# PSUM banks in rotation for Strassen products, and a longer lead of gate steps ahead of stick-breaking attention

## The chip, the cores and the metric

The kernel runs on one core of a Trainium2 chip. The metric is the device time of one execution in microseconds (us), the median of several runs; lower is better. Engines are named as the profile names them: PE is TensorE (PEld its weight loads, which run beside matmuls), DVE VectorE, ACT ScalarE, POOL GpSimd and SP SyncE.

## The reference

A decoder trunk of two layers works on one sequence of 512 positions, 2048 wide, in f32. Layer 0 is sparse attention: an indexer scores keys, the top 128 of them are kept per query, and softmax attention with 16 heads over 4 key/value groups follows, gated by SiLU. Between the layers keys and values are computed once (`shared_kv`); layer 1 attends to them by stick-breaking. Each layer ends with an output projection, a layer norm, and a gated embedding. What the change touches, cut to its core:

```python
def shared_kv(x, w_kv):
    k, v = jnp.split(x @ w_kv, [KVW_B], axis=-1)
    ...
def mixer_b(x, w_in, w_o, k, v):
    q, gate = jnp.split(x @ w_in, [WIDTH_B], axis=-1)
    ...
        z = jnp.einsum('bqngd,bsnd->bngqs', qg, k).astype(jnp.float32) * (HEAD_DIM ** -0.5)
        strict = key_pos[None, :] < t[:, None]
        log_om = jnp.where(strict, -jax.nn.softplus(z), 0.0)
        suffix = lax.cumsum(log_om, axis=log_om.ndim - 1, reverse=True) - log_om
        a = jnp.where(strict, jnp.exp(jax.nn.log_sigmoid(z) + suffix), 0.0)
        o = jnp.einsum('bngqs,bsnd->bqngd', a.astype(v.dtype), v)
    ...
    return (o * jax.nn.silu(gate)) @ w_o
```

## The kernel before, in words

**Precision.** Every f32 factor is split into a high part (rounded by ACT, `wh`, `xh`, `qh`, `sh`, `ah`) and a low part (the rest, a DVE subtraction, `wl`, `xl`, `ql`, `sl`, `al`). A product is three matmuls, high·high, high·low and low·high: `mm3`, L133, whose three matmuls carry the lines 134 to 136. Weights come by DMA from SP's queue into three buffers `raw` of two 128-row blocks each, and are split one or two blocks ahead of use (`plain_items`, L219).

**Order of work.** TensorE's instructions run in the order in which the program issues them (`manual_schedule`). On ACT and DVE a scheduler orders the instructions, except those that are pinned to the program's order. PSUM is eight banks of 128 × 512 f32, named by number through `bank(i)`, L126; a bank that is used again waits for its last reader. `interleave`, L57, mixes two generators on TensorE: first `lead` steps of the second, then, at every yield of the first, as many of the second as bring it to its share of `n_fill`; what is left comes at the end.

**Around the change.** Layer 0 ends with `finish_layer` (L731), whose embedding gate is computed in chunks of 512, 512, 256 and 256 columns, each in banks listed at L924. Then follow:

1. The keys (L970 to L974): a product of 16 k-blocks in four banks, copied by ACT into `Kf` (tile E in the profile).
2. Five chunks of Strassen products (L984 to L999), the values first and then four chunks of queries into the tiles `f`. `gemm_s` (L328) computes for each k-pair and each of two rows seven products of three 256-wide matmuls, in the bank order `M` = m1, m2, m6, m7, m5, m3, m4, one bank each; a pass over the seven products is 21 matmuls. When a chunk is done, `combine` (L351) empties the banks: ACT copies m1 (into `u`), m7 and m5, DVE adds m2 and u, m6 and u, then (a step later) the sum of the copies, m3, and m4. The next chunk's matmuls on a bank wait for that. During the second chunk the values are transposed on TensorE, four times four 128 × 128 blocks (`turn_values`, L977), in a bank that the chunk leaves free; ACT copies them back.
3. DVE and ACT split keys, values and queries (`kl`, `vl`, `ql`), and DVE makes two triangular constants (`neg`, `tri`, L1005 to L1010).
4. Four groups g of stick-breaking attention (L1113 to L1123). `sticks` (L1046) goes through ten units (i, kb) of a 128-query block and a 128-key block, each in three stages: `logits` makes z with three matmuls, softplus on ACT and DVE, and the split `sh`, `sl`; `weights` adds the suffix sums on TensorE (L1086, z from `neg`, `tri`), then exp on ACT and the split `ah`, `al`; `values` multiplies by the values into o. Step s issues logits of unit s, weights of unit s − 1, values of unit s − 2. `interleave` fills the waits with the group's gate product: 64 gate steps, one k-block and one of banks 0 to 3 each, three matmuls 512 wide (g). Group 0 has 20 gate steps ahead of its first logits and 40 more over 34 yields, the other groups 8 and 52. Behind each group ACT loads the table for SiLU, and gates.

Line 111 is the helper through which every ACT and DVE instruction goes, so the profile's groups are told apart by tile.

Of the kernel before, what the change touches and what calls it, by code (L numbers as in the profile page):

```python
# [56 lines left out]
def interleave(main, n_main, fill, n_fill, lead=0):  # L57

    steps(fill, lead)
    done = 0  # L60
    for i, _ in enumerate(main, 1):
        steps(fill, n_fill * i // n_main - done)
        done = n_fill * i // n_main
    run(fill)
# [13 lines left out]
def trunk_kernel(  # L78
# [47 lines left out]
    def bank(i, name="ps"):  # L126
        return psum.tile([128, 512], F32, name=name, tag=f"bank{i}")
# [118 lines left out]
    def gemm_w(items, get, banks, n=512, order=range(NK)):  # L246

        for i, kb in enumerate(order):
            wh, wl = next(items)
            x = get(kb)  # L250
            for j, out in enumerate(banks):
                a, b = j * 128, min(n, (j + 1) * 128)
                mm3(out[: b - a], (wh[:, a:b], wl[:, a:b]), x, i == 0, i == len(order) - 1)
                yield
# [67 lines left out]
    def strassen_stream(widths, wp):  # L322
        return Ahead(strassen_items(widths, wp), 2)

    def product_banks():
        return [bank(i, f"m{i}").rearrange("p (j t) -> p j t", j=2) for i in range(7)]

    def gemm_s(items, C3, M):  # L328

# [160 lines left out]
    items = plain_stream((512, NK, True), (80, NK, False), *[(512, NK, False)] * 11)  # L490
# [51 lines left out]
    banks = mm_banks("iq")  # L542
# [5 lines left out]
    ps = bank(7, "ik")  # L548
# [15 lines left out]
    banks = mm_banks("iq")  # L564
# [32 lines left out]
    banks = mm_banks("k")  # L597
# [52 lines left out]
    banks = [bank(b, "v") for b in (4, 5, 6, 7)]  # L650
# [11 lines left out]
    Q = split_queries(0)  # L662
# [68 lines left out]
    def finish_layer(layer, resid, last, keep, early, ahead):  # L731
# [179 lines left out]
        with tc.tile_pool(name=f"pe{layer}", bufs=1, side="right") as ep:  # L911

            def gated(n, b):
                sg = ep.tile([128, T], F32, name="sg", tag="sg", bufs=4)
                act.activation(sg, b, AF.Sigmoid)
                dve.tensor_tensor(sg, sg, E[n], ALU.mult)
                dve.tensor_tensor(fblock(n), fblock(n), sg, ALU.add)

            def store(n, k):
                rows = last[n * 128 : (n + k) * 128, :].rearrange("(j p) t -> p j t", p=128)  # L920
                nc.sync.dma_start(rows, F[n // 4][:, n % 4 : n % 4 + k])

            first = 0
            for c, (n, where) in enumerate(((512, (2, 3, 4, 5)), (512, (6, 7, 0, 1)), (256, (2, 3)), (256, (0, 1)), (0, ()))):  # L924
                for j, b in enumerate(banks):
                    bg.append(lambda n=first + j, b=b: gated(n, b))
                    if j % 2:
                        bg.append(lambda n=first + j - 1: store(n, 2))
                first += len(banks)
                if first == 12:  # L930
                    bg.extend(early)
                if not n:
                    break
                banks = [bank(b, "g") for b in where]
                gemm = pumped(gemm_w(gitems, plain, banks, n), 4 if n == 512 else 2)
                if c == 3:
                    steps(gemm, 18)
                    ahead(gemm)
                run(gemm)
                drain()  # L940
            drain()
# [25 lines left out]
    with ps_:  # L967
        sp = ps_.enter_context(tc.tile_pool(name="sp1", bufs=1))
        C3.extend(c3_tiles(sp, range(4, 8)))
        Kf, Vf = shared[0][:, 0:4], shared[0][:, 4:8]  # L970
        banks = [bank(b, "k") for b in (4, 5, 6, 7)]
        gemm = gemm_w(kitems, plain, banks, order=PAIRS)
        items = first_chunk(gemm, TF, T1, C3, lambda: strassen_stream([512] * 5, sp))
        for g in range(4):  # L974
            act.activation(Kf[:, g], banks[g], AF.Copy)

        def turn_values(t):  # L977
            s = slice(t * 128, (t + 1) * 128)
            ps = bank(7, "vt")
            for g in range(4):  # L980
                pe.transpose(ps[:, g * 128 : (g + 1) * 128], Vf[:, g, s], ident)
            act.activation(Vf[:, :, s], ps.rearrange("p (g d) -> p g d", g=4), AF.Copy)

        for n, dst in enumerate((Vf, *F)):  # L984
            M = product_banks()
            gemm = pumped(gemm_s(items, C3, M), 8)
            if n == 1:
                steps(gemm, 40)
                for t in range(4):
                    steps(gemm, 16)  # L990
                    turn_values(t)
            run(gemm)
            drain()
            if n == 4:
                for k in range(8):
                    if k % 4 == 0:
                        raw = next_raw()
                    split(XH[k][:, H:T], XL[k][:, H:T], raw[:, k % 4])
            bg.extend(combine(sp, M, lambda i: quarter(dst, i)))  # L999
        drain()  # L1000
# [31 lines left out]
    Q = split_scaled(0)  # L1032
# [13 lines left out]
    def sticks(g, Q):  # L1046
        units = [(i, kb) for i in range(4) for kb in range(i, -1, -1)]
        later = {}
        running = {}
        state = {}  # L1050
        out = {}

        def logits(u):
            i, kb = units[u]
            z = spare("z")
            ks = slice(kb * 128, (kb + 1) * 128)
            mm3(z, [k[:, ks] for k in K[g]], Q[i], True, True)
            e = work()
            keep = kb == i > 1
            sp = px.tile([128, 512], F32, name="run", tag="run", bufs=2) if keep else work()  # L1060
            act.activation(e, z, AF.Abs)
            act.activation(e, e, AF.Exp, scale=-1.0)
            act.activation(e, e, AF.Ln, bias=1.0)
            dve.scalar_tensor_tensor(sp, z, 0.0, e, ALU.max, ALU.add)
            if kb == i:
                strict(sp)
            parts = tuple(px.tile([128, 512], F32R, name=f"s{s}", tag=f"s{s}", bufs=4) for s in "hl")
            split(*parts, sp)
            state[u] = z, parts
            if keep:  # L1070
                running[i] = sp
            if kb == i:
                later[u + 1] = parts
            elif kb:
                below = tuple(px.tile([128, 512], F32R, name=f"r{s}", tag=f"s{s}", bufs=4) for s in "hl")
                dve.tensor_tensor(running[i], running[i], sp, ALU.add)
                dve.tensor_copy(below[0], running[i])
                dve.tensor_tensor(below[1], running[i], below[0].bitcast(F32), ALU.subtract)
                later[u + 1] = below

        def weights(u):
            i, kb = units[u]
            z, parts = state[u]
            terms = [(neg, p) for p in (later[u] if kb < i else ())] + [(tri, p) for p in parts]
            for n, (m, p) in enumerate(terms, 1):
                pe.matmul(z, m, p, start=False, stop=n == len(terms), skip_group_check=True)  # L1086
            a = work()
            act.activation(a, z, AF.Exp)
            if kb == i:
                strict(a)  # L1090
            parts = tuple(px.tile([128, 512], F32R, name=f"a{s}", tag=f"a{s}", bufs=2) for s in "hl")
            split(*parts, a)
            state[u] = parts

        def values(u):
            i, kb = units[u]
            if kb == i:
                out[i] = bank(7, "o")
            mm3(out[i], [v[:, g] for v in V[kb]], state.pop(u), kb == i, kb == 0)
            if kb == 0:  # L1100
                act.activation(F[g][:, :, i * 128 : (i + 1) * 128], out[i].rearrange("p (h q) -> p h q", h=4), AF.Copy)

        for s in range(12):
            for fn, u in ((logits, s), (weights, s - 1), (values, s - 2)):
                if s == 1 and fn == weights:
                    for _ in range(4):
                        yield
                if 0 <= u < 10:
                    fn(u)
                    yield  # L1110

    for g in range(4):
        tc.keep_in_program_order(act.preload_act_table_set("natural_log_exp_and_others"))  # L1113
        banks = mm_banks("g")
        interleave(sticks(g, Q), 30 + 4, gemm_w(items, plain, banks), 52 - 12 * (g == 0), lead=8 + 12 * (g == 0))
        if g < 3:
            Q = split_scaled(g + 1)
        for h in range(4):
            sg = work()
            act.activation(sg, banks[h], AF.Silu)  # L1120
            dve.tensor_tensor(F[g][:, h], F[g][:, h], sg, ALU.mult)
# [51 lines left out]
```

## Time and profile before

| what | value |
| --- | --- |
| median of 3 runs | 1927.42 us (1927.31 to 1927.74) |
| the profiled execution | 1927.01 us |
| its span in the trace | 1925.3 us |
| granted TensorE clock, mean | 0.997 |
| Strassen chunks begin at | 1066.8, 1107.1, 1150.5, 1192.0, 1233.7 us; the last ends at 1275.2 |
| group 0: first logits, last values matmuls | 1289.7, 1342.7 us |

Rows of the profile's timeline read: start, duration, engine, line, operation, written tile <- read tiles, shapes, count, and in brackets the idle time before and what ended it. A matmul's duration includes its passage through the array, and matmuls overlap, so the pitch between starts is what a matmul costs; a wait shows as a start that comes late. Rows of the waits read: the engine and its tile and line, what it waited for, and then the total, the number of times and the longest. Rows of the windows read: from and to, length, then the busy time and count of PE, PEld, DVE and ACT, the granted clock, and DMA share and rate.

### The profile page before, as it was taken

What the parts mean: (1) busy time and instruction counts of PE and PEld (TensorE: products, weight loads), DVE (VectorE), ACT (ScalarE), POOL (GpSimd) and SP (SyncE); (2) the same over time, 40 slices, a digit from 0 to 9 for tenths busy, and PEclk for the clock granted to TensorE, in tenths of its full rate; (3) what the DMA queues carried; (4) which work ended last, traced back from release to release, by engine and by line L of the source; (5) the groups of instructions that cost most, each with busy time, mean ns of one, the idle gap of its engine ahead of it and who ended that gap; (6) DMA issues with size and microseconds to landing.
All of it is one profiled execution on the core that took longest, in us unless ns stands there. A gap on an engine that the chain in (4) does not pass through costs nothing.

```text
span 1925.3 us, 25105 instructions
## 1 busy us (share of the span) xinstructions
PE 1901.7 (99%) x9223; PEld 1590.5 (83%) x9223; DVE 1226.8 (64%) x2378; ACT 932.6 (48%) x1697; POOL 45.3 (2%) x61
## 2 busy tenths in 40 slices
PE   8999999999999999999999999999999999999998
PEld 7778888888888888877888999987888888887887
DVE  6677667985566445576357788876656645568434
ACT  4345222355555433375235444458877743347323
POOL 0110000000000000000000000011100000000000
PEclk9999999999999999999999999999999999999999
DMA  6322333322222342233334333331222152242333
GB/s 195 99 77 75 93 96 98 99 77 66 66 66 67 121 142 88 88 120 112 119 112 123 106 99 100 104 116 46 70 71 64 58 180 94 81 127 88 121 99 110
DMA packets 108301, 189.24 MB, mean 98 GB/s; under 512 B 8256, under 2 KB 25664, under 8 KB 108176
## 3 DMA queue, kind: packets, MB, share of 16 engines
q1 hardware_dynamic: 108032, 187.33, 31.4%
q8 instruction: 72, 1.18, 0.3%
q14 instruction: 53, 0.43, 0.1%
q0 software_dynamic: 144, 0.30, 0.1%
HBM read 179.21 MB, written 8.39 MB: 97 GB/s over the span
## 4 chain that ended last, share of the span: by engine, by line
PE 92%; DVE 4%; ACT 1%; DMA 1%; issue 1%; POOL 0%; SPq 0%; DVEq 0%; ACTq 0%
PE g L135 12%; PE g L134 12%; PE g L136 12%; PE o L135 7%; PE o L136 7%; PE o L134 7%; PE m L134 3%; PE m L135 3%; PE m L136 3%; PE q L135 3%; PE q L136 3%; PE q L134 3%; PE z L1086 2%; PE k L135 1%; PE k L134 1%; PE k L136 1%
## 5 line engine op out<-in xcount | busy, mean ns | idle before, releaser
L111 DVE TENSOR_TENSOR wl<-raw,wh 128x512 fp32r<-128x512 f32 (+2 forms) x692 | 432.8, 627 | 469.0 <-ACT wh L111 455.1
L111 ACT ACTIVATE wh<-raw 128x512 fp32r<-128x512 f32 (+2 forms) x692 | 397.8, 576 | 678.7 <-PE g L135 245.5
L134 PE MATMUL g<-xh,wh 128*128 128x512 f32 x1024 | 404.8, 395 | 0.4 <-ACT u L111 0.3
L135 PE MATMUL g<-xl,wh 128*128 128x512 f32 x1024 | 402.0, 393 | 2.1 <-DVE xl L111 2.1
L136 PE MATMUL g<-xh,wl 128*128 128x512 f32 x1024 | 400.7, 391 | 1.3 <-DVE wl L111 1.3
L135 PEld LDWEIGHTS g<-xl,wh 128*128 128x128 f32 x1024 | 192.6, 188 | 44.7 <-DVE xl L111 6.5
L136 PEld LDWEIGHTS g<-xh,wl 128*128 128x128 f32 x1024 | 192.4, 188 | 42.2 <-DVE wl L111 1.8
L134 PEld LDWEIGHTS g<-xh,wh 128*128 128x128 f32 x1024 | 192.9, 188 | 41.5 <-ACT sg L111 1.9
L136 PE MATMUL o<-xh,wl 128*128 128x512 f32 x512 | 199.3, 389 | 0.0
L135 PE MATMUL o<-xl,wh 128*128 128x512 f32 x512 | 199.3, 389 | 0.0
L134 PE MATMUL o<-xh,wh 128*128 128x512 f32 x512 | 199.2, 389 | 0.0
L136 PEld LDWEIGHTS o<-xh,wl 128*128 128x128 f32 x512 | 96.1, 188 | 20.2 <-DVE wl L111 0.2
L135 PEld LDWEIGHTS o<-xl,wh 128*128 128x128 f32 x512 | 96.1, 188 | 20.0
L134 PEld LDWEIGHTS o<-xh,wh 128*128 128x128 f32 x512 | 96.1, 188 | 20.0
L134 PE MATMUL q<-xh,wh 128*128 128x512 f32 x256 | 99.6, 389 | 0.0
L136 PE MATMUL q<-xh,wl 128*128 128x512 f32 x256 | 99.6, 389 | 0.0
L135 PE MATMUL q<-xl,wh 128*128 128x512 f32 x256 | 99.6, 389 | 0.0
L111 ACT ACTIVATE sh<-st 128x512 fp32r<-128x512 f32 x80 | 49.9, 631 | 84.5 <-PE m L135 44.9
L111 DVE TENSOR_TENSOR sl<-st,sh 128x512 fp32r<-128x512 f32 x80 | 54.6, 689 | 38.3 <-ACT sh L111 38.3
L111 ACT ACTIVATE wk<-z 128x512 f32<-128x512 f32 x80 | 47.3, 591 | 25.8 <-PE z L136 18.6
L134 PEld LDWEIGHTS q<-xh,wh 128*128 128x128 f32 x256 | 48.1, 188 | 10.1
L135 PEld LDWEIGHTS q<-xl,wh 128*128 128x128 f32 x256 | 48.1, 188 | 9.9
(289 smaller groups left out, 3418.2 us busy)
## 6 DMA issues: line engine op xcount, KB each, us to landing
raw<-w_in_a SPq DMA_DIRECT2D x95, 512.0 KB, 3.7
raw<-w_in_b SPq DMA_DIRECT2D x64, 512.0 KB, 3.7
raw<-w_ple_gate SPq DMA_DIRECT2D x48, 512.0 KB, 3.7
raw<-w_o_a SPq DMA_DIRECT2D x24, 512.0 KB, 3.7
raw<-w_o_b SPq DMA_DIRECT2D x24, 512.0 KB, 3.8
raw<-w_ple_gate SPq DMA_DIRECT2D x32, 256.0 KB, 2.9
raw<-w_kv_b SPq DMA_DIRECT2D x16, 512.0 KB, 3.7
f<-xT SPq DMA_DIRECT2D x4, 1024.0 KB, 6.3
```

What stands on the lines that cost most here:

```text
L111: ins = method(*args, **kw)
L134: pe.matmul(out, a[0], b[0], start=start, stop=False)
L135: pe.matmul(out, a[0], b[1], start=False, stop=False)
L136: pe.matmul(out, a[1], b[0], start=False, stop=stop)
L1086: pe.matmul(z, m, p, start=False, stop=n == len(terms), skip_group_check=True)
```

## The change

It moves PSUM banks and gate steps; no arithmetic and no operation is added or taken away.

- `product_banks(first)`: a chunk's seven products lie in the banks first, first + 1, ... modulo 8, where they always lay in 0 to 6. Chunk n has first = 4 − n, so each chunk begins in the one bank that the chunk before left free: 4, 3, 2, 1, 0.
- The keys go from banks 4 to 7 to banks 0 to 3, the transposes of the values from bank 7 to bank 2, and the last two gate chunks of `finish_layer` (in both layers) from (2, 3) and (0, 1) to (4, 5) and (6, 7).
- Group 0 has 28 gate steps ahead of its first logits in place of 20, and 36 over the 34 yields in place of 40. The gate steps left behind its last values matmul are two in place of six.

In the changed program the orders of SP's and GpSimd's queues are the same as before. ScalarE's and VectorE's differ in some splits of weights inside the Strassen chunks, and in group 0: VectorE's order there is the same up to `tri`, behind which five `wl` come in place of three; at the end of the group ScalarE runs the exp of the last unit, the table load and one SiLU ahead of that unit's `ah`, where it ran exp and `ah` ahead of the table load.

```diff
-    def product_banks():
-        return [bank(i, f"m{i}").rearrange("p (j t) -> p j t", j=2) for i in range(7)]
+    def product_banks(first):
+
+        return [bank((first + i) % 8, f"m{i}").rearrange("p (j t) -> p j t", j=2) for i in range(7)]
...
-            for c, (n, where) in enumerate(((512, (2, 3, 4, 5)), (512, (6, 7, 0, 1)), (256, (2, 3)), (256, (0, 1)), (0, ()))):
+            for c, (n, where) in enumerate(((512, (2, 3, 4, 5)), (512, (6, 7, 0, 1)), (256, (4, 5)), (256, (6, 7)), (0, ()))):
...
-        banks = [bank(b, "k") for b in (4, 5, 6, 7)]
+        banks = [bank(b, "k") for b in range(4)]
...
-            ps = bank(7, "vt")
+            ps = bank(2, "vt")
...
-            M = product_banks()
+            M = product_banks(4 - n)
...
-        interleave(sticks(g, Q), 30 + 4, gemm_w(items, plain, banks), 52 - 12 * (g == 0), lead=8 + 12 * (g == 0))
+        interleave(sticks(g, Q), 30 + 4, gemm_w(items, plain, banks), 52 - 16 * (g == 0), lead=8 + 20 * (g == 0))
```

## The prediction

> **What bounds the kernel now.** I read the page's totals first, then the waits of TensorE's weight loads (a matmul's wait shows there), then the stretches around those waits engine by engine. Times are microseconds.
>
> ```profile
> span 1925.3 us, 25105 instructions
> PE 1901.7 (99%) x9223; PEld 1590.5 (83%) x9223; DVE 1226.8 (64%) x2378; ACT 932.6 (48%) x1697; POOL 45.3 (2%) x61
> ```
>
> TensorE is busy for 99% of the span, and the diff changes no arithmetic. So the change can win or lose only in what TensorE stalls, and each term below is a stall in its order of work. Two places of that order are touched: the boundaries between Strassen chunks, and group 0 of the stick-breaking stage. The waits between 1100 and 1240, where the four boundaries lie, were:
>
> ```profile
> PEld m L134 <- DVE u L111: 2.1, 4, 0.5
> PEld m L134 <- DVE f L111: 1.6, 6, 0.4
> PEld m L134 <- DVE E L111: 0.6, 2, 0.4
> ```
>
> Twelve waits, three per boundary, 4.3 in all. One boundary in full: its first 21 matmuls (seven products) and the next 21, then the additions on VectorE (DVE) that empty the old banks, then the matmuls that waited.
>
> ```profile
> 1107.10:1110.96 3.86, 3.35 (x23) 2.72 (x22) 2.25 (x4) 0.21 (x1) 1.00 0.49 136
> 1110.96:1113.47 2.51, 2.51 (x23) 2.51 (x22) 0.00 (x0) 0.00 (x0) 1.00 0.00 0
> ```
> ```profile
> 1109.18 0.68 DVE L111 TENSOR_TENSOR E<-m,E 128x512 f32<-128x512 f32 x1
> 1109.78 0.67 DVE L111 TENSOR_TENSOR E<-E,m 128x512 f32<-128x512 f32 x1
> ```
> ```profile
> 1108.38 0.39 PE L134 MATMUL m<-c3h,sh 128*128 128x256 f32 x1 [0.31 <-DVE u L111]
> ...
> 1109.92 0.38 PE L134 MATMUL m<-xh,sh 128*128 128x256 f32 x1 [0.21 <-DVE E L111]
> ...
> 1110.51 0.39 PE L134 MATMUL m<-c3h,wh 128*128 128x256 f32 x1
> ```
>
> A free pass takes 2.51, or 2.51/7 = 0.36 per product; the pass on the boundary takes 3.86, an excess of 1.35. The third, sixth and seventh product wait for the additions that read their banks; the last two start 0.06 after them (ends 1109.86 and 1110.45), the first by its row behind the addition to u. The last product takes 1110.96 − 1110.51 = 0.45 instead of 0.36, so each restart costs about 0.1 besides its wait: 12 × 0.1 + 4.3 = 5.5 for four boundaries, against 4 × 1.35 = 5.4.
>
> In group 0, the matmuls on TensorE (PE) and VectorE's queue:
>
> ```profile
> 1289.67 0.39 PE L134 MATMUL z<-qh,kh 128*128 128x512 f32 x1
> 1291.05 0.50 PE L135 MATMUL z<-ql,kh 128*128 128x512 f32 x1 [1.00 <-DVE ql L111]
> ...
> 1291.85 0.40 PE L135 MATMUL g<-xl,wh 128*128 128x512 f32 x1
> 1293.60 0.80 PE L136 MATMUL g<-xh,wl 128*128 128x512 f32 x1 [1.35 <-DVE wl L111]
> ...
> 1296.32 0.62 PE L136 MATMUL g<-xh,wl 128*128 128x512 f32 x1
> 1296.75 0.43 PE L134 MATMUL g<-xh,wh 128*128 128x512 f32 x1
> ```
> ```profile
> 1287.82 2.58 DVE L111 TENSOR_TENSOR vl<-E,vh 128x512 fp32r<-128x512 f32 x4
> 1290.32 2.48 DVE L111 SCALAR_TENSOR_TENSOR ql<-f,qh 128x512 fp32r<-128x512 f32 x4
> 1292.73 0.21 DVE L111 CAST tri<-trf 128x128 fp32r<-128x128 f32 x1
> 1292.87 1.88 DVE L111 TENSOR_TENSOR wl<-raw,wh 128x512 fp32r<-128x512 f32 x3
> ```
>
> After 20 leading gate steps (three matmuls of 0.23 each) the first logits z start at 1289.67 and wait 1.15 for ql (1291.05 − 1289.67 − 0.23), plus 0.11 of restart. Then the first step of gate block 5 waits for its weights' low half wl, which VectorE makes only after vl, ql and tri: 1293.60 − 1291.85 − 0.23 = 1.52. Behind that stall matmuls last 0.63, pitch 0.43, until 1296.75: the seven matmuls in these 3.15 take 7 × 0.227 = 1.59 at the usual pitch, so 1.56 is lost. In all 1.15 + 0.11 + 1.52 + 1.56 = 4.34 is lost here.
>
> **The change part by part.** The sum is made against the profiled execution, 1927.01 (span 1925.3 and 1.7 around it); the median of the runs is 1927.42, 0.4 above, which is added at the end.
>
> *Strassen banks.* Each chunk starts in the bank left free, so product i+1 takes the bank of old product i: every wait moves one product, 0.36, later, and the last bank (m4's) is wanted by no one until the next chunk. VectorE's order of these additions is the same in the changed program. With the rows above: the fourth product is due at 1107.10 + 3 × 0.36 = 1108.18 and waits to 1108.38 (0.20 + 0.10); the seventh is due at 1108.38 + 0.10 + 1.08 = 1109.56 and waits to 1109.92 (0.36 + 0.10). 0.76 in place of 1.35: 0.6 saved, four times, **−2.4**. Bounds: 0 (the additions are later by as much) and −5.4 (all waits gone). I take −2.4, worked out from this boundary's own rows.
>
> *Costed at nothing.* Keys in banks 0 to 3: chunk 0 then begins in bank 4, so again four free banks come first and its fifth product takes the first key bank. The two 256-wide gate chunks of both layers go to the banks left by a chunk one before the last. The transposes of the values go to bank 2, the free one of that chunk; this asks for cover, because the next chunk begins there: behind the last transposes come 8 steps of three matmuls, 24 × 0.12 (2.51/21) = 2.9, and ScalarE's copy out of the bank takes 0.60 (row below), so ScalarE would have to come 2.3 late. The last chunk lies in banks 0 to 6 as before, so the gate's own banks come free as before. The reordered weight splits inside a chunk are due over a us later. If a cover failed it would be a restart and a wait of under 1.
>
> ```profile
> 1147.79 0.60 ACT L111 ACTIVATE E<-vt 128x512 f32<-128x512 f32 x1
> ```
>
> *Eight more leading steps.* No engine's queue puts block 5's wl ahead of vl, ql and tri: VectorE's order up to tri is the same, after it now come five wl in place of three. TensorE comes to block 5 earlier, straight after step 20: its third matmul is due at 1289.67 + 0.46 = 1290.13, and the first wl behind tri lands at 1293.55 (1292.87 and 0.68 for one such pass), just before that matmul's row. One stall of 3.47 replaces 1.15 + 0.11 + 1.52 = 2.78: **+0.7**. Cover for ql is now complete. The fall of the clock behind it I leave at its 1.56.
>
> *The chain z to sl.* The eight steps are taken from those between and behind the units, and these were what hid ScalarE's and VectorE's work:
>
> ```profile
> PEld z L1086 <- DVE sl L111: 1.4, 3, 0.6
> PEld o L135 <- DVE al L111: 0.8, 2, 0.6
> ```
> ```profile
> 1353.40 0.39 PE L136 MATMUL z<-qh,kl 128*128 128x512 f32 x1
> ```
> ```profile
> 1359.04 0.68 DVE L111 TENSOR_TENSOR sl<-wk,sh 128x512 fp32r<-128x512 f32 x1
> ```
>
> These waits are those of group 0 (1289 to 1345). The two rows are group 1, where TensorE ran at full clock: from the last matmul of z to the end of sl 6.32. In group 0 unit 0 now has 23 matmuls in that place instead of 26, 5.3, so it waits 1.0 and restarts, 1.2 where it lost some 0.45 (1.4 / 3): **+0.8**. Units 3 and 9, the other two of the row of three, had no slack and lose three matmuls too, 0.69 each: **+1.4**. Units 6 to 8 lose three as well; they did not wait before. Bounds: 0 for all (splits come earlier because weights do) and +4.3 (all six lose 0.69 or 0.8).
>
> *The tail.*
>
> ```profile
> 1340.76 0.60 ACT L111 ACTIVATE wk<-z 128x512 f32<-128x512 f32 x1 [0.69 <-PE z L1086]
> 1341.39 0.63 ACT L111 ACTIVATE ah<-wk 128x512 fp32r<-128x512 f32 x1
> ...
> 1345.38 1.28 ACT L111 ACT_TABLE_LOAD   x1
> 1346.67 1.58 ACT L111 ACTIVATE wk<-g 128x512 f32<-128x512 f32 x3
> ```
> ```profile
> 1342.65 0.40 PE L134 MATMUL o<-ah,vh 128*128 128x512 f32 x1
> ```
>
> Two gate steps instead of six are left behind the last values matmul, so the gate's first bank is done earlier, and ScalarE's order changes: exp of unit 9, then the table load (1.28) and one Silu (0.60), only then ah. ah comes 1.88 later. The last values matmul began at 1342.65, 0.63 after ah ended, so it waits 1.25, and al, a further VectorE pass of 0.68 behind ah, waits about 0.5 more with its restart: **+1.9**. Bounds: 0 and +2.5. [...]
>
> Sum: −2.4 + 0.7 + 0.8 + 1.4 + 1.9 = **+2.4**: 1929.4 in the profiled execution's frame, **1929.8** in the median's.
>
> **The rivals.**
>
> *R1, slower: the clock falls a second time.* Place: the last values matmul of group 0. Price: the 1.56 of the fall at 1293.60, so 1931.4. For it:
>
> ```profile
> 125.32 0.38 PE L582 MATMUL isc<-B,sb 128*128 128x256 f32 x1 [1.89 <-ACT rl L111]
> ...
> 126.18 0.63 PE L136 MATMUL k<-xh,wl 128*128 128x512 f32 x1
> ```
>
> A wait of 1.89 was followed by a matmul of 0.63. It decides from about 1.9 of idle time close together; the tail has 1.25 and 0.5, one matmul between them. Against it: the boundary's twelve waits, none over 0.5, kept a clock of 1.00, and nothing shows what 1.25 alone does.
>
> *R2, faster: the eight steps do cover.* If block 5's wl is ready when TensorE comes to it (the splits run earlier than VectorE's order says), the whole 4.34 goes, and +0.7 with it: −4.34 − 2.4 + 0.8 + 1.4 + 1.9 = −2.6, 1924.8. Against it: VectorE has no gap between 1287.82 and 1294.75, and wl stands last in it.
>
> *R3: the clock holds at the long stall.* Then 1.56 is saved: 1928.2. The row at 1293.60 fell after waits of 1.00 and 1.35 with four matmuls between; the new stall is whole. [...]
>
> *R4: the change of banks doesn't do what it says*, gaining half or less because the additions follow TensorE: +1.2, 1931.0.
>
> **How the numbers follow.** Forecast 0.44, R1 0.22, R3 0.16, R2 0.11, R4 0.07. What can be told from no change here is 0.2%, 3.85: under 1923.57 is faster, over 1931.27 slower. The forecast's own range is 1927.6 (the units cost nothing) to 1931.9 (all six lose) and holds 0.08 above the bound; R1 0.13 above and 0.09 below; R4 0.04 and 0.03; R3 within; R2 0.06 faster and 0.05 within. So faster 0.06, within 0.69, slower 0.25. The range leaves out R2 below and the top of R1 with the longer bounds of the units above: 1926.0 to 1932.6.
>
> **What would show it.** At the boundaries: two waits instead of three, on the fourth and the seventh product, and a pass near 3.3. At the first gate step of block 5: one wait of about 3.4 on wl, then matmuls of 0.63. No wait of z on ql. sl waits in units 0, 3 and 9, about 1 each. A table load between exp and ah at the end of group 0 and a wait of 1.2 there. Wrong if wl of block 5 lands before 1291, if a boundary pass is 2.5 or 3.8, or if new waits stand where I put none, such as the transposes' bank.

## The result and the profile after

The changed kernel takes 1931.34 us (median of 17 runs, 1930.06 to 1932.92) against 1926.76 for the kernel before (17 runs, 1925.40 to 1929.06): ratio 1.0024, 95% interval 1.0017 to 1.0031, so **4.6 us slower**. The prediction had 1929.8, range 1926.0 to 1932.6, and 2.4 slower. The profiled execution took 1932.92, its page beginning:

```profile
span 1931.2 us, 25094 instructions
...
PE 1903.3 (99%) x9223; PEld 1589.8 (82%) x9223; DVE 1228.4 (64%) x2378; ACT 932.1 (48%) x1697; POOL 45.9 (2%) x61
```

In the code after, lines from 326 on are one further down, so L1086 is now L1087. The waits of TensorE's weight loads at the four Strassen boundaries (1100 to 1240), and the first two passes over the seven products at the first boundary:

```profile
PEld m L134 <- DVE f L111: 1.1, 3, 0.4
PEld m L134 <- DVE u L111: 1.0, 4, 0.3
PEld m L134 <- DVE E L111: 0.4, 1, 0.4
```
```profile
1108.33:1111.61 3.28, 3.03 (x24) 2.63 (x23) 2.18 (x4) 0.20 (x1) 1.00 0.53 160
1111.61:1114.12 2.51, 2.51 (x23) 2.51 (x22) 0.08 (x1) 0.00 (x0) 1.00 0.00 0
```

Eight waits of 2.5 in all stand where there were twelve of 4.3, and the pass takes 3.28 where it took 3.86: 0.58 gained at this boundary, as forecast. VectorE's additions stay where they were: the first of the two that the prediction shows starts 2.08 behind the boundary (1110.41 − 1108.33), as it did before (1109.18 − 1107.10).

```profile
1110.41 0.68 DVE L111 TENSOR_TENSOR E<-m,E 128x512 f32<-128x512 f32 x1
```

Over the whole stage, from the start of the first Strassen matmul to that of the last, this trace takes 206.11 (1068.01 to 1274.12) where the first trace of before took 208.44 (1066.79 to 1275.23): 2.33 gained. Below, **excess** is the time by which the starts of matmuls come later than at the usual pitch (0.227 for 512 columns: in before 13 matmuls, each a row of 0.39, take from the start at 1286.72 to that at 1289.67), added up over a wait or a stretch.

Group 0 is where the time went. TensorE and VectorE there:

```profile
1288.79 0.39 PE L135 MATMUL g<-xl,wh 128*128 128x512 f32 x1
1292.50 0.79 PE L136 MATMUL g<-xh,wl 128*128 128x512 f32 x1 [3.32 <-DVE wl L111]
1293.09 0.63 PE L134 MATMUL g<-xh,wh 128*128 128x512 f32 x1
...
1297.78 0.57 PE L136 MATMUL g<-xh,wl 128*128 128x512 f32 x1
1298.20 0.39 PE L134 MATMUL g<-xh,wh 128*128 128x512 f32 x1
```
```profile
1286.72 2.58 DVE L111 TENSOR_TENSOR vl<-E,vh 128x512 fp32r<-128x512 f32 x4
1289.22 2.48 DVE L111 SCALAR_TENSOR_TENSOR ql<-f,qh 128x512 fp32r<-128x512 f32 x4
1291.63 0.21 DVE L111 CAST tri<-trf 128x128 fp32r<-128x128 f32 x1
1291.77 1.88 DVE L111 TENSOR_TENSOR wl<-raw,wh 128x512 fp32r<-128x512 f32 x3
```

VectorE's four rows are those of before, all 1.1 earlier. TensorE comes to block 5 at 1289.02 and waits there once, 3.48 (1292.50 − 1288.79 − 0.23), for the same wl for which it waited 1.15 + 0.11 + 1.52 before. Behind it the matmuls of 0.63 last until 1298.20, 5.70 instead of 3.15. The waits of the stage (1280 to 1355), with the columns total, times, longest:

```profile
PEld g L136 <- DVE wl L111: 3.7, 1, 3.7
PEld z L1087 <- ACT sh L111: 2.8, 3, 1.0
PEld z L1087 <- DVE sl L111: 2.2, 4, 0.7
PEld o L134 <- ACT ah L111: 1.8, 2, 1.5
PEld o L135 <- DVE al L111: 1.4, 3, 0.6
```

The wait on ql is gone; waits on sh, the high half, are new, at units 0, 3 and 9, where the prediction named sl alone. ScalarE (ACT) around unit 9 and the end of the group:

```profile
1344.98 0.63 ACT L111 ACTIVATE wh<-raw 128x512 fp32r<-128x512 f32 x1
1345.52 0.61 ACT L111 ACTIVATE sh<-wk 128x512 fp32r<-128x512 f32 x1
1347.53 0.60 ACT L111 ACTIVATE wk<-z 128x512 f32<-128x512 f32 x1 [1.40 <-PE z L1087]
1348.15 1.28 ACT L111 ACT_TABLE_LOAD   x1
1349.44 0.60 ACT L111 ACTIVATE wk<-g 128x512 f32<-128x512 f32 x1
1349.94 0.62 ACT L111 ACTIVATE ah<-wk 128x512 fp32r<-128x512 f32 x1
```
```profile
1350.61 0.49 PE L134 MATMUL o<-ah,vh 128*128 128x512 f32 x1 [1.02 <-ACT ah L111]
1351.34 0.49 PE L135 MATMUL o<-al,vh 128*128 128x512 f32 x1 [0.23 <-DVE al L111]
```

exp at 1347.53, the table load and one SiLU, then ah: the order that was read from the changed program. The SiLU starts 1.29 after the load does (1349.44 − 1348.15), as it did before (1346.67 − 1345.38).

### The profile page after: what moved, and what is told of

Its sections match the earlier page's. It is cut to its first block, busy times and chain, and to the rows that moved or that the text cites. A ratio compares the mean times of both kernels' runs of the same rounds, so it can differ in the third digit from the quotient of the medians.

```text
span 1931.2 us, 25094 instructions
## 1 busy us (share of the span) xinstructions
PE 1903.3 (99%) x9223; PEld 1589.8 (82%) x9223; DVE 1228.4 (64%) x2378; ACT 932.1 (48%) x1697; POOL 45.9 (2%) x61
## 5 line engine op out<-in xcount | busy, mean ns | idle before, releaser
L134 PE MATMUL iq<-xh,wh 128*128 128x512 f32 x128 | 51.0, 398 | 5.6 <-ACT wh L111 5.5
L136 PEld LDWEIGHTS q<-xh,wl 128*128 128x128 f32 x256 | 48.0, 188 | 10.1
```

The costliest lines, as they stand in the source:

```text
L134: pe.matmul(out, a[0], b[0], start=start, stop=False)
L136: pe.matmul(out, a[1], b[0], start=False, stop=stop)
```

## The experiments

**Theory** after the result: the banks gain 2.4; the eight steps cost it back threefold, because (a) block 5's wl stands behind vl, ql and tri in VectorE's order, (b) the steps are missing where they hid ScalarE and VectorE, and (c) the table load slips ahead of the last ah. **Rivals**: part of the loss is the banks'; wl is late for another reason; the tail waits in any order. Times of a run are compared with runs of the kernel before on the same chip.

**e1, the banks alone.** All of the diff but its last line.

> The change of banks alone (keys, gate chunks, transposes and Strassen chunks as after the change; group 0 keeps 20 leading gate steps and 40 over the yields). Theory: each chunk boundary loses 0.77 in two waits in place of 1.35 in three, so the waits of the four boundaries add up to 2.5 in place of 4.3 and the time falls by 2.4 us against the kernel before. Group 0 as before: waits of 1.15 on ql and 1.5 on wl, no wait at the last values matmul. Rival: the additions that empty the banks follow TensorE, so the waits move without shrinking: 0 to -1 us.

Measured: 1923.91 against 1925.83, −1.9 (ratio 0.9992, interval 0.9983 to 1.0000). The interval reaches up to no change, so the time alone does not show the gain; the trace does. Its waits between 1100 and 1260 are, line for line, the three of the changed kernel above, and its Strassen stage takes 206.11 (1066.25 to 1272.36), 2.33 less than before. The rival falls: the additions do not follow TensorE.

**e2, the lead alone.** The diff's last line on the kernel before.

> The eight leading gate steps alone, banks as before. Theory: all of the loss comes from group 0, whose stalls grew by 6.8 us between the two traces: +5.7 to +7 us against the kernel before, by how long the clock stays down behind the stall on wl (1.6 to 2.7 us lost). One stall of 3.5 on wl of gate block 5, waits in units 0, 3 and 9 of 1.3 each, 1.8 at the last values matmul. Rival: part of the loss comes from the banks (the transposes' bank, the gate's banks): then it is under +4 us.

Measured: 1933.19 against 1925.83, +7.4 (1.0036, 1.0024 to 1.0049), a little above the upper end. In group 0 its five rows of waits are those of the changed kernel but for the first, 3.8 in place of 3.7. With e1 on the same chip: −1.9 + 7.4 = +5.5, where the whole change measured +4.6 with an interval of 3.3 to 6.0. So these runs leave no part of the loss to the banks.

**e3, ah ahead of the table load.** The changed kernel with

```diff
-            split(*parts, a)
+            ah = act.activation(parts[0], a, AF.Copy)
+            last[:] = [ah.ins]
+            dve.tensor_tensor(parts[1], a, parts[0].bitcast(F32), ALU.subtract)
...
-            act.activation(sg, banks[h], AF.Silu)
+            with tc.issue_after(last[0]):
+                act.activation(sg, banks[h], AF.Silu)
```

> The changed kernel with one order fixed on ScalarE: the SiLU of a group is issued behind the last unit's ah, so that the table load comes behind ah as it did before. Theory: the wait of 1.2 on ah and 0.6 on al at the last values matmul is the table load's and SiLU's 1.88: it falls to under 0.2, and the time is 1.6 to 1.8 us below the changed kernel (+2.8 against before where the change as a whole is +4.6). Rival: without those six gate steps behind it ah would be late in any order (exp waits for the sums): the wait stays at 0.6 or more and under 1 us is won.

Measured: 1929.70 against 1925.83, +3.9 (1.0017, 1.0009 to 1.0026) where +2.8 was expected. That is 1.6 less than e1 and e2 add up to, but only 0.7 less than the +4.6 of the whole change, and the intervals overlap: the times do not decide between theory and rival. The trace does. In its waits of group 0 the row of ah is down from 1.8 to 0.4, and what is left of it is unit 0's:

```profile
PEld o L135 <- DVE al L111: 1.0, 3, 0.6
PEld o L134 <- ACT ah L111: 0.4, 1, 0.4
```

The last three values matmuls start at 1346.70, 1346.93 and 1347.19, late by 0.03 in all. So it was ScalarE's order, not the lack of steps behind the group.

**e5, the weights' low halves first.** Banks as after, 20 leading steps and 40 over the yields, and in VectorE's order the wl of blocks 5 and 6 ahead of vl and the last two ql, the casts of the other keys behind them. `late_split` is `split` with its ScalarE half in the program's order:

```diff
-    split(*K[0], Kf[:, 0])
-    for t in range(4):
-        split(*V[t], Vf[:, :, t * 128 : (t + 1) * 128])
...
-    Q = split_scaled(0)
...
+    gate = gemm_w(items, plain, first_banks)
+    steps(gate, 12)
+    split(*K[0], Kf[:, 0])
+    Q = split_scaled(0, (0, 1))
+    pinned[0] = True
+    steps(gate, 20 - 12)
+    for t in range(4):
+        late_split(*V[t], Vf[:, :, t * 128 : (t + 1) * 128])
+    Q += split_scaled(0, (2, 3), nc.scalar)
     for g in range(1, 4):
         split_dve(*K[g], Kf[:, g], pool)
+    pinned[0] = False
...
```

> Banks as after the change, 20 leading gate steps and 40 over the yields as before, and VectorE's order changed: the low halves of gate blocks 5 and 6 come ahead of the values' and the last two query blocks' low halves, and the casts of the other three key blocks come behind these. Theory: the waits on ql and wl at the start of group 0 come from VectorE's order alone, and the clock falls because of them: both waits and the fall go (1.15, 0.11, 1.52 and 1.56 us), the time is 4.3 us below e1, some 6.7 below the kernel before; new waits may appear at z of unit 0, whose softplus now shares VectorE with the work put behind: up to 2 us back. Rival: the weights' low half is late because its high half or its transfer is late: the wait on wl stays over 1 us.

Measured: 1929.46 against 1925.83, +3.6 (1.0017, 1.0008 to 1.0026) where −6.7 was expected: a miss. The first half held, both waits on ql and wl are gone from the trace, so VectorE's order alone made them. But unit 0 then waited 6.89 for sh. The three rows that lead there, of ScalarE, GpSimd and TensorE:

```profile
1295.72 0.60 ACT L111 ACTIVATE wk<-z 128x512 f32<-128x512 f32 x1 [4.19 <-POOL kl L1018]
```
```profile
1289.86 5.83 POOL L1018 TENSOR_TENSOR kl<-E,kh 128x512 fp32r<-128x512 f32 x3 [8.96 <-DVE kh L111]
```
```profile
1300.01 0.79 PE L1099 MATMUL z<-sh,tri 128*128 128x512 f32 x1 [6.89 <-ACT sh L111]
```

ScalarE's first step on z writes a buffer wk. The pool of wk was given the place of tile E, which held the keys and the values and was closed just ahead (`pk_.close()`), so wk waits until E has been read for the last time. Here that was GpSimd's kl: it began its 5.83 of subtractions only when VectorE had made the casts that I had put last. This is a dependency through memory, which no engine's order shows.

**e6, the other keys early.** As e5, with the casts of the three key blocks and GpSimd's subtractions ahead of the pinned part (`with tc.issue_after(mask.ins)` around their loop, so that GpSimd makes the mask for tri first).

> As e5_defer20, but the casts of the other three key blocks and GpSimd's subtractions for them (5.8 us, behind the mask that tri is made of) stay early, ahead of the last gate blocks' low halves. Theory: the wait of 7 us in unit 0 of e5 came from ScalarE's first step on z, which needs buffers that lie where the keys lay and so waits for GpSimd's subtractions; with these early the wait falls to under 1, the waits on ql and wl stay gone, and the time is 1.5 to 4 us below the change of banks alone (e1), 4 to 6 below the kernel before. Rival: the order put VectorE behind, so unit 0 waits 2 us or more for sl and the time is that of e1 or above.

Measured: 1923.45 against 1926.64, −3.2 (0.9985, 0.9976 to 0.9994), less than the 4 to 6 expected. The wait fell, but to 1.92, not under 1: ScalarE now waited for VectorE's vl, the last to read E. TensorE's rows come first, then ScalarE's:

```profile
1295.63 0.62 PE L1100 MATMUL z<-sh,tri 128*128 128x512 f32 x1 [1.92 <-ACT sh L111]
1296.35 0.79 PE L1100 MATMUL z<-sl,tri 128*128 128x512 f32 x1
1296.94 0.63 PE L134 MATMUL g<-xh,wh 128*128 128x512 f32 x1
```
```profile
1290.92 0.60 ACT L111 ACTIVATE wk<-z 128x512 f32<-128x512 f32 x1 [1.98 <-DVE vl L111]
```

**e7, the change's 28 and 36 steps on e6.**

> As e6_kearly20 with 28 leading gate steps and 36 over the yields, as in the change. Theory: with wl ready in time the eight steps themselves still cost what they take from the units and the tail: 1.2 to 1.4 us in each of units 0, 3 and 9 where there were 0.1 to 0.4, and 1.8 at the last values matmul: 4 to 5 us above e6. No long stall on wl and no fall of the clock. Rival: with wl in time the eight steps cover the chain of unit 0: within 1 us of e6.

Measured: 1925.19 against 1926.64, −1.5 (0.9991, 0.9983 to 1.0000), and 1.7 above e6: neither the 4 to 5 of the theory nor within 1. Both hold in part. Unit 0's loss falls from 2.57 and the clock's 1.5 to 0.94: with wl in time the eight steps do cover it. Units 3 and 9 lose 1.28 and 1.40 and the tail 1.78, within 0.01 of what they lose in the changed kernel.

**e8 and e9, the two kernels once more, for the clock.**

> The kernel before once more, for the clock behind the two waits at the start of group 0. Theory: the clock is decided in fixed windows of 3.413 us; it falls at a window's end when some 60% of it or more was idle, and the two waits (2.4 idle in 3.5 us) fill so much of one window only if it lies just over them, in about 1 trace of 5: most likely no fall here, as in e1. Rival: the fall follows the waits, whatever the time: matmuls of 0.63 behind 1293, as in the first trace.

> The changed kernel once more, for the clock. Theory of fixed windows: the one wait of 3.5 us fills 60% of a window in about 5 cases of 6, so the clock falls again and stays down for one window or two (3.4 or 6.8 us less what lies inside the stall); the rise lies a whole number of 3.413 us behind the rise near 130. Rival: the time that the clock is down follows the length of the stall and is 5.7 us, as in the first trace.

e8 took 1925.27 and its clock held behind the same two waits; e9 took 1931.08 and its clock fell, but the slow matmuls last 3.76 (1291.76 to 1295.52) and not 5.70 behind a stall of the same length:

```profile
1290.92 0.50 PE L135 MATMUL z<-ql,kh 128*128 128x512 f32 x1 [1.01 <-DVE ql L111]
...
1293.46 0.50 PE L136 MATMUL g<-xh,wl 128*128 128x512 f32 x1 [1.33 <-DVE wl L111]
1293.80 0.40 PE L134 MATMUL z<-qh,kh 128*128 128x512 f32 x1
```
```profile
1291.76 0.60 PE L136 MATMUL g<-xh,wl 128*128 128x512 f32 x1 [3.34 <-DVE wl L111]
1292.16 0.63 PE L134 MATMUL g<-xh,wh 128*128 128x512 f32 x1
...
1295.15 0.53 PE L135 MATMUL g<-xl,wh 128*128 128x512 f32 x1
1295.52 0.40 PE L136 MATMUL g<-xh,wl 128*128 128x512 f32 x1
```

Among the traces with the waits of before (the first, e1, e8) it fell in one of three; among those with the one long stall (after, e2, e3, e9) in four of four.

**e10 and e11, a lead between the two, with all of it in order.** e6 with 24 (e11: 22) leading steps, still 40 over the yields, and e3's order of ah and SiLU.

> As e6_kearly20, with 24 leading gate steps, still 40 over the yields (so none is left behind the group), and SiLU issued behind the last unit's ah as in e3_tail. Theory: four more steps ahead of z cover what unit 0 still waited for in e6 (2.1 and the clock behind it, 1.5), units 3 and 9 keep their steps and wait as little as in e6, and with ah ahead of the table load the tail needs no steps behind it: 3 to 4 us below e6, 6 to 7 below the kernel before. Rival: the eight steps of the change cost their time because the tail must have steps behind the last values matmul: then 1 to 2 us are lost there and the time is at most 2 below e6.

> As e10_lead24 with 22 leading steps, two left behind the group. Theory: unit 0 waits 0.5 to 1 longer than in e10, not enough idle for the clock to fall; within 1 us of e10. Rival (unit 0 is as late after z whatever the lead, because the order of VectorE and ScalarE sets it): the same wait of unit 0 in e10, e11 and e6.

Measured: e10 1921.37 against 1926.37, **−5.0** (0.9972, 0.9962 to 0.9983), the fastest of all; against the changed kernel 10.0 less by the two medians. Its waits in group 0 (1280 to 1345) are:

```profile
PEld z L1102 <- DVE sl L111: 1.8, 4, 0.6
PEld o L135 <- DVE al L111: 0.7, 2, 0.5
```

This falls short of the 6 to 7 expected. It is 1.8 below e6, which is where the rival put the time (at most 2), but not for the rival's reason: the last values matmuls wait for nothing in the trace. One reason can be read from the runs: e6's trace has a fall of the clock behind unit 0, worth 1.5, but 4 of its 11 executions had a mean clock of 1.000, which leaves no room for one (3.41 us at a clock of 0.50, as in the last section, would take 0.0009 off the mean), so the fall is not in every time to be won. The rest stays open. e11 took 1923.05, −3.3 (0.9983, 0.9974 to 0.9992): 1.7 above e10, not within 1. In its trace unit 0 loses 1.76 and the clock holds; in e10 unit 0 loses 0.27. So the wait does depend on the lead, and the rival falls.

## Why the prediction was right, point by point

The sign and the range were right: slower by a little, inside 1926.0 to 1932.6, with the gain at the banks and the loss in group 0 as two separate sums. The sum was 2.2 short. The terms, as excess in the first two traces (before to after) and in e8 and e9:

| term | predicted | first pair | e8 to e9 |
| --- | --- | --- | --- |
| Strassen boundaries | −2.4 | −2.3 | −2.3 |
| stall on wl of block 5, with ql's before | +0.7 | 2.78 to 3.48, +0.7 | 2.78 to 3.50, +0.7 |
| clock behind it | 0 | 1.56 to 2.75, +1.2 | 0.11 (a restart) to 1.72, +1.6 |
| unit 0 | +0.8 | 0.42 to 1.33, +0.9 | 0.42 to 1.33, +0.9 |
| units 3 and 9 | +1.4 | 0.43 to 2.68, +2.25 | 0.44 to 2.68, +2.2 |
| tail | +1.9 | 0 to 1.78, +1.8 | 0 to 1.78, +1.8 |

The 1.72 of e9, for example, is 1295.52 − 1291.76 = 3.76 for nine matmuls that take 9 × 0.227 = 2.04 at the usual pitch. With 0.2 at units 6 to 8 the terms add up to some 4.7 and 5.1. The spans of the pairs are 5.9 and 5.8 apart, but of this 1.2 and 0.6 have arisen ahead of the first Strassen matmul (1066.79 to 1068.01, and 1066.64 to 1067.25). Traces differ as much there without any change in that stretch (1068.01 in after, 1066.25 in e1, which has the same change ahead of it), so this is not counted as the change's.

**Banks.** "Every wait moves one product" was right to the row: two waits at each boundary, a pass of 3.28 against 3.86. The costs of nothing held: the transposes' bank, the keys and the gate chunks show no wait.

**The stall.** One stall of 3.47 was worked out from VectorE's order and TensorE's due time; 3.48 came. e5 shows its cause by taking it away.

**The clock: the step that failed.** "The fall of the clock behind it I leave at its 1.56" took the fall of the one trace at hand as a fixture of the kernel before. It is not: in two of three traces with the same waits it did not happen. The kernel before ran 66 more times beside the experiments. In 21 of these its mean granted clock was 0.997, as in the first trace, where the clock fell twice (near 126 and here); in 38 it was 0.999 or 1.000, as in e8. Their medians are 1927.5 and 1925.7. The change made a fall that came in some executions into one that came in each of four traces, for 1.7 to 2.75. That is 1.2 of the 2.2 missing in the first pair, and more where the clock had held before.

**Units 3 and 9: mis-sized.** Three matmuls fewer, 0.69 each, was right; the rest was ScalarE's order, which I did not look at for these units. At unit 9 the changed order has wh ahead of sh (rows above), where sh came first before; at unit 3 the absolute value of the next z, which waits for TensorE, comes ahead of sh, where it came behind it before. Unit 3 after the change, then units 3 and 9 before:

```profile
1318.21 0.60 ACT L111 ACTIVATE wk<-z 128x512 f32<-128x512 f32 x1 [0.63 <-PE z L136]
1318.70 0.62 ACT L111 ACTIVATE sh<-run 128x512 fp32r<-128x512 f32 x1
```
```profile
1312.01 0.63 ACT L111 ACTIVATE sh<-run 128x512 fp32r<-128x512 f32 x1 [1.33 <-POOL run L1044]
1312.55 0.58 ACT L111 ACTIVATE wk<-z 128x512 f32<-128x512 f32 x1
...
1338.74 0.62 ACT L111 ACTIVATE sh<-wk 128x512 fp32r<-128x512 f32 x1
1339.44 0.63 ACT L111 ACTIVATE wh<-raw 128x512 fp32r<-128x512 f32 x1
```

At unit 3 run was ready at 1318.36 and sh began 0.34 later; at unit 9 wh took 0.54 (1344.98 to 1345.52) ahead of sh. Some 0.3 and 0.6 were missing from the forecast at these two units. No run reversed these two orders alone, so this is read from the rows and not tried. Units 6 to 8 cost 0.2 of the 2.1 that stood as their bound.

**The rivals.** R1, a second fall at the tail, did not come: 1.02 and 0.23 idle were too little, in after, e2, e7 and e9 alike. R2 fell: wl was late by VectorE's order. R3 fell in four traces of four. R4 fell by e1's trace, in which the stage is 2.33 shorter. The two rivals on the clock reasoned from one stall's length, where the last section shows that in these traces it was its place as well.

## What to carry to other kernels

Work put ahead of a stall as cover does not cover it when the work itself waits for the same engine (here eight gate steps, and 2.78 of waiting became 3.48): look where in that engine's queue its inputs stand, and reorder the queue first. A term that one trace shows once, a fall of the clock above all, is a chance and not a constant (here it fell in one of three traces with the same waits), and two more traces of the kernel before would have told so. When steps are moved, read every engine's order in each place from which they are taken; over a third of the loss in group 0 (1.8 + 0.9 of 7) went with orders that a scheduler chose: a table load, as e3 shows, and two swaps, as the rows suggest.

## What the runs showed of the hardware

**TensorE's granted clock changed on a grid of 3.41 us in these traces.** Cut where the granted clock changes, the trace of after reads as follows (from and to, length, TensorE's busy time and count, granted clock, then the DMAs):

```profile
1287.93:1291.34 3.41, 1.25 (x6) 1.00 0.00 0
1291.34:1294.75 3.41, 2.25 (x5) 0.50 0.31 68
1294.75:1298.17 3.42, 3.42 (x9) 0.50 0.73 238
```

A window, below, is such a stretch of 3.41. In this trace the clock rises at 130.81 and at 1298.17, 1167.36 = 342.0 × 3.413 apart. In the first trace of before the rises at 129.44 and 1296.80 are 1167.36 apart as well; in e5 those at 128.42 and 1306.02 are 1177.60 = 345.0 windows apart; in e9 those at 8.61 and 1295.43 are 1286.82 = 377.0.

With the windows counted on from a rise in each trace, the clock fell behind windows in which TensorE stood idle for 1.88 (e7, near 126, 55%), 1.92 (e6, 56%), 2.14 (before), 2.16 (after, the first row), 2.53 (e3), 2.66 (e5), 3.15 (e9) and 3.21 (e2), and it held behind all with less, up to 1.84 (e11, near 126, 54%). The ends of matmuls are modelled in the profile, so the bound in these traces is no sharper than "somewhat over half". Some 60%, which e8's theory took, was too high: 55% by this count was enough. A wait of 1.9 near 125, the row that R1 quotes, makes the phase plain: the clock fell behind it in the seven traces in which one window held the whole wait, and not in the five in which an edge cut it. In e8 an edge lay between the two waits of group 0, and each window had 1.17 idle:

```profile
1288.88:1292.29 3.41, 2.24 (x9) 1.00 0.00 0
1292.29:1295.70 3.41, 2.24 (x10) 1.00 0.32 72
```

So waits of 1.01 and 1.33 with 1.2 of work between them cost 0.11 more in e8, and waits of 1.00 and 1.35 cost 1.56 more in the first trace, where one window (1289.97 to 1293.38) held 2.14 of idle time. In after, the window behind the fall still had 1.16 of the stall in it and the clock stayed down for a second one, 6.83 in all (1291.34 to 1298.17).

**In two runs a wait came through memory.** In e5 and e6 ScalarE waited 4.19 and 1.98 for engines whose results it did not read, because its output took the place of a tile that they were still reading.
